# Norms between the stages of a two-layer encoder: other places for their rows, four buffers, an earlier transpose, a later weight load

## The chip, the core and the metric

The kernel runs on one core of a Trainium2 chip. The metric is the device time of one execution in microseconds; less is better. TensorE multiplies, VectorE and ScalarE do the elementwise work, GpSimd some of it, and SyncE issues most of the transfers. TensorE's clock has two levels here, 2.4 GHz (a granted clock of 1.00 in the profile) and 1.2 GHz (0.50).

## The reference

Two layers over 512 tokens of width 1024. Each layer has three parts, each behind a norm, each added to x. Layer 0 ends in a dense SwiGLU, layer 1 in eight experts of which each token takes two.

```python
for l in range(DEPTH):
    h = rms_norm(x, norm_mix[l])
    cols_a, cols_b, gate_a, gate_b = split_cols(h @ w_in[l], IN_SIZES)
    y_a, v_first = rwkv7_branch(cols_a, ...)      # time mixing, 8 heads
    y_b = dsa_attention(...)                      # top-128 sparse attention, 8 heads
    merged = (sigmoid(gate_a) * (y_a @ w_branch_a[l]) + sigmoid(gate_b) * (y_b @ w_branch_b[l]))
    x = x + merged @ w_out[l]
    x = x + memory_attention(rms_norm(x, norm_mem[l]), rms_norm(mem, mem_tok_norm[l]), ...)
    h = rms_norm(x, norm_ffn[l])
    x = x + (swiglu(h, ...) if l % 2 == 0 else moe_swiglu(h, router, bias, ...))
```

## The kernel before

Tokens lie in four tiles of 128 (`t` 0 to 3). Every float32 operand of a product is split into two float16 parts, a high one (`whi`, `hh`, `qhl`, `mh`, `oh`) and a low one (`wlo`, `hl`, `ml`, `ol`), and a product is three passes: low part of x times high of w, high times high, high times low. A weight tile goes through `wtile` (L251): SyncE loads it raw (L259), ScalarE casts the high part (L266), VectorE forms the low part (L271). Loads share a small ring of raw buffers, and SyncE takes its transfers in order: a transfer that waits for its place holds up the ones behind it.

`norm_T` (L167) is the norm between two stages. For each token tile ScalarE squares the rows of x and sums them (L182; the squares themselves go into the tile `xs` and are thrown away), VectorE and GpSimd make the scale factor `rs` (L164, L165), VectorE writes the scaled rows into the same `xs` (L187), and TensorE transposes them in 8 blocks of 128 by 128 into `pT` (L193), from which ScalarE and VectorE cast the two parts (L201, L202). `xs` has two buffers.

The stages around it, in order: `resid` (L1090) multiplies the merged branches (`mh`, `ml`) by w_out with `proj_tok` (L314, products at L331) and adds the result to x (L1096). `proj_tok` takes the last part of the weights token tile by token tile, so that x is complete for tile 0 first and for tile 3 last. `mem_attn` (L1156) then norms x, projects the queries of heads 0 and 1 with `proj_first` (L292, products at L301, the first 256 tokens ahead of the others), and runs the four heads; its output projection mem_wo adds to x at L1227. In layer 0 the projections of the memory tokens for layer 1 (`mem_kv`, weights mem_wkv) run in between. Then comes `ffn` (L1248) in layer 0 and `moe` (L1275) in layer 1, each with its norm. In `moe` the scaled rows are kept: `norm_T` puts them into tiles `row0` to `row3` of a pool, ScalarE makes their high part, GpSimd (VectorE for the last) the low part `rowl` (L1313), and `route` (L1381) makes the router's scores `plog`, the ranking `prk` and the gathering `px`.

The code is written as generators, and a scheduler orders each engine's instructions by their dependences and planned times; what the code fixes by hand, it fixes with `order` (L309): one instruction behind another on the same engine, without a wait. `self.hold`, where it is set, puts every weight load behind the load `self.lastw` of that moment. It is set to w_out's last load before the memory attention (L1739), and cleared after it.

Places in the on-chip memory are shared by pools that follow each other, and a tile that is laid on an older one waits until that one has been read. Before the change, in both layers, the second and the third raw buffer of the memory attention lie on `ml`, which w_out's products read to their end. The first of the expert layer's rows lies on `ol`, which mem_wo's products read to their end.

Of the kernel before, what the change touches and what calls it, by code (L numbers as in the profile page):

```python
# [8 lines left out]
F32 = mybir.dt.float32  # L9
# [3 lines left out]
F16 = mybir.dt.float16  # L13
# [6 lines left out]
P = 128  # L20
SEQ = 512
D = 1024
KT = 8
NT = 4
# [30 lines left out]
class Kern:  # L55
# [110 lines left out]

    def norm_T(self, xt, nt, targets, hd=None, rows=None, spread=False, gbs=None):  # L167

        nc = self.nc
        kept = []
        with self.tc.tile_pool(name="norm", bufs=2, side="right", reuse_waits="tile") as pn:
            gbs = gbs or [self.spread(g, f"gb{i}", pn) if spread else self.bcast_vec(g, D, f"gb{i}", pn)
                          for i, (g, _, _) in enumerate(targets)]
            for t in range(nt):
                ts = slice(t * P, (t + 1) * P)
                ssq = pn.tile([P, 1], F32, name="ssq")
                rs = pn.tile([P, 1], F32, name="rs")
                xs = pn.tile([P, D], F32, name="xs") if rows is None else rows.tile([P, D], F32, name=f"row{t}")  # L180
                kept.append(xs)
                nc.scalar.activation(xs, xt[:, t, :], AF.Square, accum_out=ssq)  # L182
                self.rstd(ssq, rs, 1, 1.0 / D, EPS)
                for i, (_, hi, lo) in enumerate(targets):
                    if i:
                        xs = pn.tile([P, D], F32, name="xs")
                    nc.vector.scalar_tensor_tensor(xs, xt[:, t, :], rs, gbs[i], OP.mult, OP.mult)  # L187
                    if hd is not None:
                        nc.scalar.dma_start(hd[ts, :], xs)
                    for q in range(2):  # L190
                        p = self.sm("pT")
                        for k in range(4):
                            nc.tensor.transpose(p[:, k * P:(k + 1) * P], xs[:, (4 * q + k) * P:(4 * q + k + 1) * P], self.ident)  # L193
                        ks = slice(4 * q, 4 * q + 4)
                        self.split_ps(hi[:, ks, ts], lo[:, ks, ts], p.rearrange("p (k t) -> p k t", k=4))
        return kept
# [117 lines left out]
    def proj_tok(self, pieces, xh, xl, nt, kt=KT, tail=1, tag="acc", kg=None):  # L314


        N = sum(p.shape[1] for p in pieces)
        kg = kg or max(1, 1024 // N)
        while kt % kg:
            kg -= 1  # L320
        ps = [self.bank(tag, "ptok") for _ in range(nt)]
        mm = self.nc.tensor.matmul
        groups = list(range(0, kt, kg))
        cut = max(0, len(groups) - tail)
        for part in [[k0] for k0 in groups[:cut]] + [groups[cut:]]:
            ws = [(k0, self.wtile([pc[k0 * P:(k0 + kg) * P, :] for pc in pieces], kg)) for k0 in part]
            for t in range(nt):
                ts = slice(t * P, (t + 1) * P)
                for k0, (hi, lo) in ws:
                    for k, x, w, first, last in self.passes(range(kg), xh, xl, hi, lo):  # L330
                        mm(ps[t][:, :N], lhsT=x[:, k0 + k, ts], rhs=w[:, k, :], start=k0 == 0 and first,  # L331
                           stop=k0 + kg == kt and last)
        return [p[:, :N] for p in ps]

# [718 lines left out]
    def branches(self, l, pool, G, ya, ybd, cx, ms):  # L1053


        nc, I = self.nc, self.I
        mf = self.hp.tile([P, KT, SEQ], F32, name="mf", tag="hl", bufs=1)
        for m in range(KT):
# [5 lines left out]
            yield  # L1064
        mp = cx.enter_context(self.tc.tile_pool(name="branch", bufs=1, reuse_waits="tile"))
        yb = mp.tile([P, 8, SEQ], F16, name="yb", tag="yb")
        for i in range(2):
            nc.sync.dma_start(yb[:, 4 * i:4 * i + 4, :], ybd[i].rearrange("j p t -> p j t"))
        ybl = [[yb[:, 4 * i + j, :] for j in range(4)] for i in range(2)]
        for m in range(KT):  # L1070
            tb = mp.tile([P, SEQ], F32, name="tb", bufs=3)
            nc.sync.dma_start(tb, G[8 + m])
            pb = self.proj_feat(I["w_branch_b"][l][:, m * P:(m + 1) * P], *ybl, 4)
            nc.vector.scalar_tensor_tensor(tb, tb, 1.0, pb, OP.add, OP.mult)
            nc.gpsimd.tensor_tensor(mf[:, m, :], mf[:, m, :], tb, OP.add)
            yield
# [3 lines left out]
        for m in range(KT):  # L1080
            ta = mp.tile([P, SEQ], F32, name="ta", bufs=7)
            nc.sync.dma_start(ta, G[m])
            pa = self.proj_feat(I["w_branch_a"][l][256:512, m * P:(m + 1) * P], [y[0] for y in ya[2:4]],
                                [y[1] for y in ya[2:4]], 2)
            nc.vector.scalar_tensor_tensor(ta, ta, 1.0, pa, OP.add, OP.mult)
            nc.vector.tensor_tensor(ta, ta, mf[:, m, :], OP.add)
            self.split_ps(mh[:, m, :], ml[:, m, :], ta, 0.5 / SW)
            yield
# [67 lines left out]
    def mem_attn(self, l, x, kv):  # L1156
# [5 lines left out]
        with self.more_weights(3, 3, 3), tc.tile_pool(name="mattn", bufs=1, reuse_waits="tile") as mp:  # L1162
            oh = mp.tile([P, 4, SEQ], F16, name="oh")
            ol = mp.tile([P, 4, SEQ], F16, name="ol")
            self.norm_T(x, NT, [(I["norm_mem"][l], hh, hl)])
            kT = mp.tile([P, 2, 4, 256], F16, name="akT")
# [81 lines left out]
    def ffn(self, l, x):  # L1248
        nc, I, tc = self.nc, self.I, self.tc
        hh = self.hp.tile([P, KT, SEQ], F16, name="fh", tag="hh", bufs=1)  # L1250
        hl = self.hp.tile([P, KT, SEQ], F16, name="fl", tag="hl", bufs=1)
        self.norm_T(x, NT, [(I["norm_ffn"][l], hh, hl)])
        j = l // 2
# [21 lines left out]
    def moe(self, l, x, out, c2, rawp):  # L1275
# [7 lines left out]
        with ExitStack() as cx:  # L1283
# [23 lines left out]
            ld[0] = itertools.chain([next(ld[0]) for _ in range(self.RAWS)], ld[0])  # L1307
            with self.psum(acc=4, sm=4), tc.tile_pool(name="router", bufs=1, reuse_waits="tile") as rp:
                hr = [rp.tile([P, NT, D], F16, name=f"row{c}") for c in "hl"]
                rows = self.norm_T(x, NT, [(I["norm_ffn"][l], hh, hl)], hd, rp)  # L1310
                for t, r in enumerate(rows):
                    a = nc.scalar.copy(hr[0][:, t, :], r).ins
                    (nc.vector if t == NT - 1 else nc.gpsimd).tensor_tensor(hr[1][:, t, :], r, hr[0][:, t, :], OP.subtract)  # L1313
                self.order(a, self.marks["hi"])
                self.marks["rows"] = a
                self.route(l, rp, hh, hl, hr, slot, gate, ovf, S7, XTs[0])
            with self.psum(acc=6, sm=2):
# [62 lines left out]

    def route(self, l, rp, hh, hl, hr, slot, gate, ovf, S7, XT):  # L1381

# [6 lines left out]
        sh = [P, NT, E]  # L1389
        rr = rp.tile([P, KT, E], F32, name="rr")  # L1390
        rs = rp.tile([P, KT, 2, E], F16, name="rs")
        rb = self.bcast_vec(I["moe_bias"][j], E, "rb", rp)
        nc.scalar.dma_start(rr, I["moe_router"][j].rearrange("(k p) e -> p k e", p=P))
# [302 lines left out]
    def layer(self, l, xsrc, xs):  # L1696
# [38 lines left out]
        with tc.tile_pool(name="memkv", bufs=1, side="right", reuse_waits="tile") as mp:  # L1735
# [6 lines left out]
            if l % 2 == 0:  # L1742
                self.mem_attn(l, x, kv)
                self.hold = None
        if l % 2:
# [10 lines left out]
        self.weights(*self.WB[2])  # L1756
        self.ffn(l, x)
        px.close()
        xd = self.dp.tile([SEQ, D], F32, name=f"xe{l}")
# [45 lines left out]
```

## Time and profile before

| | |
|---|---|
| median of 3 executions | 2080.55 us (2078.53 to 2082.65) |
| profiled execution | 2075.39 us, its span 2073.6 us |
| TensorE | busy 94% of the span, mean granted clock 0.959 |
| VectorE, ScalarE, GpSimd | busy 68%, 50%, 16% |

The times in the rows below are from the start of that span. Layer 0 ends its w_out at 564 and its memory attention near 660; layer 1 runs from there, with its w_out near 1526, its mem_wo near 1598, and the experts from 1620 to the end. The columns of each view are explained with its first group. In brackets at the end of a row of a timeline stands the idle time of that engine ahead of the row and what ended it.

### The profile page before, as it was taken

To read this page: it belongs to the slowest core of one execution; us is meant where nothing else is said; L and a number is where in the kernel's file an instruction comes from. 1 tells how busy PE (TensorE), PEld (TensorE's weight loads), DVE (VectorE), ACT (ScalarE), POOL (GpSimd) and SP (SyncE) were. 2 spreads that over 40 slices of the span, in tenths; PEclk is the share of its full clock that TensorE was granted. 3 is DMA by queue.
4 is the path that set the end of the run, shared out by engine and by line. 5 is a ranking of instruction groups with operands and counts; after the bars stand their busy time and mean duration, and the time that the engine had idled before them with its cause. 6 is when DMAs were issued, how large, how long until landed. Compare 5 with 4: busy or idle time off the path is not lost.

```text
span 2073.6 us, 40817 instructions
## 1 busy us (share of the span) xinstructions
PE 1940.1 (94%) x16760; PEld 1286.0 (62%) x16760; DVE 1413.4 (68%) x2373; ACT 1029.1 (50%) x1661; POOL 341.0 (16%) x357
## 2 busy tenths in 40 slices
PE   6998899899898999999998989979998899999997
PEld 3764565465465444444574546537455799999996
DVE  6766987756676333322466998574757888888886
ACT  5543446453453333322443435544335678888883
POOL 2260611003010000000243260100201310000002
PEclk9998999979999999999999999988999899999998
DMA  7334334325642333333434342434535699999993
GB/s 234 106 80 99 87 90 127 97 64 159 221 147 62 102 102 102 102 102 102 121 81 94 89 120 65 120 99 130 173 114 202 189 394 365 356 355 347 345 344 127
DMA packets 346742, 332.52 MB, mean 160 GB/s; under 512 B 101921, under 2 KB 263841, under 8 KB 346546
## 3 DMA queue, kind: packets, MB, share of 16 engines
q1 hardware_dynamic: 335440, 306.03, 47.2%
q10 hardware_dynamic: 8482, 15.39, 2.0%
q0 software_dynamic: 2624, 8.40, 1.2%
q8 instruction: 133, 2.18, 0.4%
q14 instruction: 63, 0.52, 0.1%
HBM read 297.05 MB, written 32.72 MB: 159 GB/s over the span
## 4 chain that ended last, share of the span: by engine, by line
PE 70%; DVE 12%; DMA 7%; ACT 3%; issue 3%; POOL 3%; SPq 2%; DVEq 0%; ACTq 0%; POOLq 0%
PE pf L289 23%; PE ptok L331 12%; PE pe L1567 10%; PE py L1612 6%; PE pSy L904 3%; PE pf L301 3%; PE ptok L349 2%; PE psc L527 1%; DVE wlo L271 1%; DMA eraw<-in_moe_wd_dram 1%; DVE iacc L518 1%; DVE pr L1003 1%; PE pA L808 1%; PE pT L193 1%; PE pp L558 1%
## 5 line engine op out<-in xcount | busy, mean ns | idle before, releaser
L266 ACT ACTIVATE whi<-raw 128x1024 f16<-128x1024 f32 (+2 forms) x244 | 227.7, 934 | 436.9 <-PE pf L289 187.3
L271 DVE SCALAR_TENSOR_TENSOR wlo<-raw,whi 128x1024 f16<-128x1024 f32 (+2 forms) x210 | 232.0, 1107 | 201.7 <-ACT whi L266 190.3
L1550 DVE SCALAR_TENSOR_TENSOR ewlo<-eraw,ewhi 128x1024 f16<-128x1024 f32 x265 | 321.1, 1220 | 58.0 <-ACT ewhi L1549 56.7
L289 PEld LDWEIGHTS <-whi 128*128 128x128 f16 x1888 | 182.5, 99 | 229.5 <-issue 34.8
L1549 ACT ACTIVATE ewhi<-eraw 128x1024 f16<-128x1024 f32 x265 | 277.4, 1054 | 77.9 <-PE py L1612 34.6
L1567 PE MATMUL pe<-XT,ewhi 128*128 128x144 f16 x2816 | 206.3, 226 | 1.7 <-issue 1.7
L1567 PEld LDWEIGHTS <-ewhi 128*128 128x128 f16 x2816 | 183.4, 98 | 2.3 <-issue 1.6
L289 PE MATMUL pf<-hh,whi 128*128 128x512 f16 x448 | 171.7, 383 | 2.6 <-DVE v L613 1.0
L289 PE MATMUL pf<-hl,whi 128*128 128x512 f16 x448 | 171.5, 383 | 0.0
L289 PEld LDWEIGHTS <-wlo 128*128 128x128 f16 x944 | 92.4, 99 | 112.0 <-issue 9.0
L269 POOL TENSOR_TENSOR wlo<-raw,whi 128x1024 f16<-128x1024 f32 (+3 forms) x34 | 59.9, 1761 | 596.1 <-ACT raw L268 512.9
L289 PE MATMUL pf<-fh,whi 128*128 128x512 f16 x336 | 127.3, 379 | 0.0
L289 PE MATMUL pf<-fl,whi 128*128 128x512 f16 x336 | 127.3, 379 | 0.0
L1567 PE MATMUL pe<-XT,ewlo 128*128 128x144 f16 x1408 | 117.2, 226 | 0.1
L289 PE MATMUL pf<-hh,wlo 128*128 128x512 f16 x448 | 112.6, 386 | 0.0
L1612 PE MATMUL py<-HT,ewhi 128*128 128x144 f16 x1408 | 103.9, 227 | 0.1
L1567 PEld LDWEIGHTS <-ewlo 128*128 128x128 f16 x1408 | 94.3, 98 | 0.8 <-issue 0.7
L1612 PEld LDWEIGHTS <-ewhi 128*128 128x128 f16 x1408 | 92.5, 98 | 0.3 <-issue 0.2
L289 PE MATMUL pf<-fh,wlo 128*128 128x512 f16 x336 | 79.4, 379 | 0.0
L349 PE MATMUL ptok<-whi,hh 128*128 128x256 f16 (+1 forms) x320 | 74.7, 274 | 2.1 <-ACT qe L485 2.0
L349 PE MATMUL ptok<-whi,hl 128*128 128x256 f16 (+1 forms) x320 | 75.0, 274 | 0.0
L349 PEld LDWEIGHTS <-hh 128*128 128x128 f16 x640 | 62.4, 100 | 15.5 <-issue 8.2
(462 smaller groups left out, 3879.3 us busy)
## 6 DMA issues: line engine op xcount, KB each, us to landing
raw<-in_w_in_dram SPq DMA_DIRECT2D x76, 512.0 KB, 4.0
eraw<-in_moe_wg_dram SPq DMA_DIRECT2D x16, 2048.0 KB, 12.9
eraw<-in_moe_wu_dram SPq DMA_DIRECT2D x16, 2048.0 KB, 14.3
eraw<-in_moe_wd_dram SPq DMA_DIRECT2D x16, 2048.0 KB, 12.9
eraw<-in_moe_wg_dram SPq DMA_DIRECT2D x8, 1536.0 KB, 11.9
eraw<-in_moe_wu_dram SPq DMA_DIRECT2D x8, 1536.0 KB, 14.6
eraw<-in_moe_wd_dram SPq DMA_DIRECT2D x8, 1536.0 KB, 8.5
raw<-in_ffn_wg_dram SPq DMA_DIRECT2D x22, 512.0 KB
```

Source lines behind the costliest of these rows:

```text
L266: nc.scalar.activation(hi, raw, AF.Copy, scale=SW)
L269: nc.gpsimd.tensor_tensor(lo, raw, hi, OP.subtract)
L271: nc.vector.scalar_tensor_tensor(lo, raw, SW, hi, OP.mult, OP.subtract)
L289: self.nc.tensor.matmul(p, lhsT=w[:, k, :], rhs=x[k], start=first, stop=last)
L301: m = self.nc.tensor.matmul(ps[i][:, cs], lhsT=w[:, k, :], rhs=x[k][:, cs], start=hf == 0 and start, stop=stop, skip_group_check=True)
L331: mm(ps[t][:, :N], lhsT=x[:, k0 + k, ts], rhs=w[:, k, :], start=k0 == 0 and first, stop=k0 + kg == kt and last)
L349: mm(p, lhsT=x[:, k0 + k, ts], rhs=w[:, k, :], start=k0 == 0 and t % 2 == 0 and first, stop=k0 + kg == kt and last, skip_group_check=True)
L904: m = mm(p[e][:, cc % 4, jj, :], lhsT=l, rhs=r, start=first[e] is None, stop=x == (1 if cc else 0), skip_group_check=True)
L1549: a = nc.scalar.activation(r[0], w, AF.Copy, scale=SW)
L1550: d = nc.vector.scalar_tensor_tensor(r[1], w, SW, r[0], OP.mult, OP.subtract)
L1567: mm(p[:, i * n:(i + 1) * n], lhsT=w[:, k, :], rhs=XT[:, k, h, :], start=z == 0, stop=z == len(ms) - 1)
L1612: mm(ps[d], lhsT=w[:, i, d * P:(d + 1) * P], rhs=HT[:, k, h, :], start=k == 0 and w is wh and h == 0 and d % per == 0, stop=k == FT - 1 an ...
```

## The change

- `norm_T` takes the number of `xs` buffers: four for the memory attention's norm in both layers and for the SwiGLU's norm in layer 0. It also takes `ahead`, instructions that are ordered behind the 8 transposes of the token tiles 0, 1, ... The memory attention gives it the first product of token tile 3 in w_out's last part (`self.tails[3:4]`, recorded by `proj_tok`).
- In `branches` the first of the tiles `tb` and `ta` are allocated ahead of `yb`, whose place `ml` takes later. `ml` thereby moves, and the raw buffers of the memory attention lie on `tb` and `ta`, which nobody reads by then.
- In `moe` the rows, their gain, and the router's tiles get a pool of their own on the right side. The gain vector `gbr` is loaded by SyncE behind the first four expert loads; it was loaded long before.
- `self.hold` isn't cleared after layer 0's memory attention but set to its last load, so that the SwiGLU's first weight loads stand behind mem_wo's.

```diff
-    def norm_T(self, xt, nt, targets, hd=None, rows=None, spread=False, gbs=None):
+    def norm_T(self, xt, nt, targets, hd=None, rows=None, spread=False, gbs=None, bufs=2, ahead=()):
...
-                xs = pn.tile([P, D], F32, name="xs") if rows is None else rows.tile([P, D], F32, name=f"row{t}")
+                xs = pn.tile([P, D], F32, name="xs", bufs=bufs) if rows is None else rows.tile([P, D], F32, name=f"row{t}")
...
-                            nc.tensor.transpose(p[:, k * P:(k + 1) * P], xs[:, (4 * q + k) * P:(4 * q + k + 1) * P], self.ident)
+                            m = nc.tensor.transpose(p[:, k * P:(k + 1) * P], xs[:, (4 * q + k) * P:(4 * q + k + 1) * P], self.ident)
+                        if t < len(ahead):
+                            self.order(ahead[t], m.ins)
...
+            self.tails = []
             for t in range(nt):
...
-                        mm(ps[t][:, :N], lhsT=x[:, k0 + k, ts], rhs=w[:, k, :], start=k0 == 0 and first,
+                        m = mm(ps[t][:, :N], lhsT=x[:, k0 + k, ts], rhs=w[:, k, :], start=k0 == 0 and first,
                            stop=k0 + kg == kt and last)
+                        if len(self.tails) == t:
+                            self.tails.append(m.ins)
...
+        tbs = [mp.tile([P, SEQ], F32, name="tb", bufs=3)]
+        tas = [mp.tile([P, SEQ], F32, name="ta", bufs=7)]
         yb = mp.tile([P, 8, SEQ], F16, name="yb", tag="yb")
...
-            tb = mp.tile([P, SEQ], F32, name="tb", bufs=3)
+            tb = tbs.pop() if tbs else mp.tile([P, SEQ], F32, name="tb", bufs=3)
...
-            ta = mp.tile([P, SEQ], F32, name="ta", bufs=7)
+            ta = tas.pop() if tas else mp.tile([P, SEQ], F32, name="ta", bufs=7)
...
-            self.norm_T(x, NT, [(I["norm_mem"][l], hh, hl)])
+            self.norm_T(x, NT, [(I["norm_mem"][l], hh, hl)], bufs=4, ahead=self.tails[3:4])
...
-        self.norm_T(x, NT, [(I["norm_ffn"][l], hh, hl)])
+        self.norm_T(x, NT, [(I["norm_ffn"][l], hh, hl)], bufs=4)
...
+                rwp = cx.enter_context(ExitStack())
+                rw = rwp.enter_context(tc.tile_pool(name="rows", bufs=1, side="right", reuse_waits="tile"))
+                gb = self.bcast_vec(I["norm_ffn"][l], D, "gbr", rw)
                 hr = [rp.tile([P, NT, D], F16, name=f"row{c}") for c in "hl"]
-                rows = self.norm_T(x, NT, [(I["norm_ffn"][l], hh, hl)], hd, rp)
+                rows = self.norm_T(x, NT, [(I["norm_ffn"][l], hh, hl)], hd, rw, gbs=[gb])
...
-                self.route(l, rp, hh, hl, hr, slot, gate, ovf, S7, XTs[0])
+                self.route(l, rp, rw, hh, hl, hr, slot, gate, ovf, S7, XTs[0])
+                rwp.close()
...
-        rr = rp.tile([P, KT, E], F32, name="rr")
-        rs = rp.tile([P, KT, 2, E], F16, name="rs")
-        rb = self.bcast_vec(I["moe_bias"][j], E, "rb", rp)
+        rr = rw.tile([P, KT, E], F32, name="rr")
+        rs = rw.tile([P, KT, 2, E], F16, name="rs")
+        rb = self.bcast_vec(I["moe_bias"][j], E, "rb", rw)
...
                 self.mem_attn(l, x, kv)
-                self.hold = None
+                self.hold = self.lastw
...
         self.ffn(l, x)
+        self.hold = None
```

TensorE at the end of w_out in layer 0, before: `ptok` are w_out's products for token tile 3, `pT` the transposes of the norm, `pf` the first query products.

```order
L331 LDWEIGHTS mh
L331 MATMUL ptok<-wlo,mh 128x512
L331 LDWEIGHTS mh
L331 MATMUL ptok<-wlo,mh 128x512
L193 MATMUL pT<-ct,xs 128x128 x24
L301 LDWEIGHTS whi
L301 MATMUL pf<-qhl,whi 128x256
```

The same place after: the last products of token tile 2, the transposes of tile 0, and the first products of tile 3.

```order
L334 LDWEIGHTS mh
L334 MATMUL ptok<-wlo,mh 128x512
L193 MATMUL pT<-ct,xs 128x128 x8
L334 LDWEIGHTS mh
L334 MATMUL ptok<-whi,mh 128x512
```

The transposes of tile 0 moved ahead of the 12 products of tile 3; behind these stand the 16 transposes of tiles 1 and 2, then 16 query products, then the 8 transposes of tile 3, where all of the first three tiles' transposes stood behind the products before.

ScalarE in the second half of layer 0's memory attention, before: `aq` is the last head's copy of its queries, `apr` its softmax, `oh` the head outputs, `whi<-raw` the cast of a weight tile.

```order
L204 ACTIVATE aqT<-pf 128x512
L204 ACTIVATE apT<-pmt 128x512 x2
L1178 ACTIVATE aq_6526<-pf 128x512
L204 ACTIVATE oh<-pmo 128x512
L1203 ACTIVATE apr,asm<-pms,amx,aqs 128x256 x2
L204 ACTIVATE apT<-pmt 128x512
L1203 ACTIVATE apr,asm<-pms,amx,aqs 128x256 x2
L266 ACTIVATE whi<-raw 128x512
```

The same place after; the casts of 128x1024 here are of the SwiGLU's first weights.

```order
L206 ACTIVATE aqT<-pf 128x512
L206 ACTIVATE apT<-pmt 128x512 x2
L268 ACTIVATE whi<-raw 128x1024
L1185 ACTIVATE aq_6526<-pf 128x512
L206 ACTIVATE oh<-pmo 128x512
L268 ACTIVATE whi<-raw 128x1024 x2
L1210 ACTIVATE apr,asm<-pms,amx,aqs 128x256 x4
L268 ACTIVATE whi<-raw 128x512
```

Three SwiGLU casts now stand here, ahead of the last head's query copy and softmax; before, they ran on ScalarE during w_out and the norm behind it. On SyncE the SwiGLU's loads stand behind the fifth load of mem_wo now, and the small loads of layer 1's constants (`mu` and others, L589) behind them; before, the SwiGLU's first five loads stood among those of w_out, mem_wq and mem_wkv.

VectorE in the middle of layer 1, inside the last inverse of the time mixing (`pr` and `tt` are its steps; L986, L987), before: `wlo` is the low part of a weight tile, `rv` the reciprocal of a softmax sum.

```order
L986 TENSOR_TENSOR pr<-tt_12566,Bt 128x49
L271 SCALAR_TENSOR_TENSOR wlo<-raw,whi 128x1024
L987 TENSOR_REDUCE tt_12566<-pr 128x7
L986 TENSOR_TENSOR pr<-tt_12566,Bt 128x64
L987 TENSOR_REDUCE tt_12566<-pr 128x8
L986 TENSOR_TENSOR pr<-tt_12566,Bt 128x81
L546 RECIPROCAL rv<-sme 128x4
```

The same steps after: `mf` is a gate product, `ybl` the low part of the sparse attention's output, the two lines of L546 one score pass of the sparse attention.

```order
L991 TENSOR_TENSOR pr<-tt_12566,Bt 128x49
L273 SCALAR_TENSOR_TENSOR wlo<-raw,whi 128x256
L992 TENSOR_REDUCE tt_12566<-pr 128x7
L1068 SCALAR_TENSOR_TENSOR mf<-gt,pf 128x512
L207 SCALAR_TENSOR_TENSOR ybl<-po,ybh 128x256
L991 TENSOR_TENSOR pr<-tt_12566,Bt 128x64
L546 ISA s_13045,mx<-psc,mask_9209 128x512
L546 ISA mx 128x1
L546 ISA s_13045,mx<-psc,mask_9209 128x512
L546 ISA mx 128x1
L992 TENSOR_REDUCE tt_12566<-pr 128x8
L991 TENSOR_TENSOR pr<-tt_12566,Bt 128x81
```

Gate products and score passes moved between the inverse's steps; before, most of them stood behind them.

## Rows read from the trace of the kernel before

**Rows 1.** The page, chain that ended last: share of the span by engine

```profile
PE 70%; DVE 12%; DMA 7%; ACT 3%; issue 3%; POOL 3%; SPq 2%; DVEq 0%; ACTq 0%; POOLq 0%
```

**Rows 2.** Timeline of TensorE at A: start, us, engine, line, operation, out<-in, count, idle before

```profile
564.03 1.91 PE L193 MATMUL pT<-ct,xs 128*128 128x128 f32 x16
569.64 1.94 PE L193 MATMUL pT<-ct,xs 128*128 128x128 f32 x8 [3.70 <-DVE xs L187]
...
579.16 0.38 PE L331 MATMUL ptok<-whi,memh 128*128 128x512 f16 x1
```

**Rows 3.** Windows: length, busy us (instructions) of PE, PEld, DVE, ACT, POOL; PEclk, DMA share, GB/s

```profile
568.00:569.00 1.00, 0.00 (x0) 0.00 (x0) 0.79 (x1) 1.00 (x3) 0.18 (x1) 0.50 0.94 332
...
574.00:575.00 1.00, 1.00 (x7) 0.74 (x6) 1.00 (x2) 0.00 (x0) 0.00 (x0) 0.61 0.92 244
...
636.00:640.00 4.00, 4.00 (x15) 2.04 (x13) 3.92 (x11) 1.83 (x6) 0.00 (x0) 0.57 0.62 132
```

**Rows 4.** Timeline of ScalarE at A: square of tile 2, a SwiGLU cast, two query casts

```profile
566.10 1.08 ACT L182 ACTIVATE xs<-x 128x1024 f32<-128x1024 f32 x1
...
567.15 1.06 ACT L266 ACTIVATE whi<-raw 128x1024 f16<-128x1024 f32 x1
...
569.62 2.14 ACT L266 ACTIVATE whi<-raw 128x1024 f16<-128x1024 f32 x2
```

**Rows 5.** Timeline of VectorE at A: second half of tile 2's sum, its scaled rows

```profile
561.80 0.68 DVE L1096 SCALAR_TENSOR_TENSOR x<-ptok,x 128x512 f32<-128x512 f32 x1
...
568.21 1.28 DVE L187 SCALAR_TENSOR_TENSOR xs<-x,rs,gb 128x1024 f32<-128x1024 f32 x1 [0.73 <-POOL rs L165]
```

**Rows 6.** Timelines of ScalarE and TensorE at D: query casts, transposes of tile 2

```profile
1530.80 2.02 ACT L266 ACTIVATE whi<-raw 128x1024 f16<-128x1024 f32 x2
...
1531.95 1.94 PE L193 MATMUL pT<-ct,xs 128*128 128x128 f32 x8 [3.87 <-DVE rs L164]
```

**Rows 7.** Timelines of all engines at E, from the last output product on

```profile
1598.18 1.06 ACT L182 ACTIVATE row<-x 128x1024 f32<-128x1024 f32 x1 [8.09 <-PE ptok L331]
...
1600.20 1.28 DVE L187 SCALAR_TENSOR_TENSOR row<-x,rs,gb 128x1024 f32<-128x1024 f32 x1 [0.69 <-POOL rs L165]
...
1601.63 1.42 PE L193 MATMUL pT<-ct,row 128*128 128x128 f32 x8 [3.54 <-DVE rs L164]
...
1604.06 2.64 POOL L1313 TENSOR_TENSOR rowl<-row,rowh 128x1024 f16<-128x1024 f32 x1 [1.36 <-ACT rowh L1312]
1607.18 5.20 POOL L1313 TENSOR_TENSOR rowl<-row,rowh 128x1024 f16<-128x1024 f32 x2
1607.24 3.14 DVE L187 SCALAR_TENSOR_TENSOR row<-x,rs,gb 128x1024 f32<-128x1024 f32 x1
...
1610.53 1.94 PE L193 MATMUL pT<-ct,row 128*128 128x128 f32 x8 [1.98 <-DVE lg L1403]
```

**Rows 8.** Timeline at C: a wait of VectorE, and TensorE's first row behind it

```profile
634.14 0.17 DVE L594 TENSOR_SCALAR mu<-mu 128x14 f32<-128x14 f32 x1 [3.12 <-DMA mu<-in_rwkv_mu_dram]
...
634.97 0.39 PE L331 MATMUL ptok<-whi,ol 128*128 128x512 f16 x1 [2.62 <-DVE ol L205]
```

**Rows 9.** Timeline of SyncE's queue: the five loads of mem_wo

```profile
605.68 17.53 SPq L259 DMA_DIRECT2D raw<-in_mem_wo_dram  x5
```

**Rows 10.** Timeline of layer 1's middle, around the last inverse

```profile
1364.84 0.68 DVE L541 CUSTOM_DVE_ANT_0 s<-psc,mask 128x512 f32<-128x512 f32 x1
...
1371.14 1.89 DVE L1003 TENSOR_TENSOR pr<-t1h,a 128x1024 f32<-128x1024 f32 x1 [5.62 <-DMA scrT<-tt]
...
1378.33 1.54 PE L558 MATMUL pp<-ct,s 128*128 128x128 f32 x6 [8.22 <-DVE mx L541]
...
1384.99 0.69 DVE L1063 SCALAR_TENSOR_TENSOR mf<-gt,pf 128x512 f32<-128x512 f32 x1 [0.63 <-DMA gt<-gatebuf]
```

**Rows 11.** Windows of layer 1's middle, ahead of the first scan

```profile
1200.00:1220.00 20.00, 13.04 (x82) 8.75 (x81) 19.34 (x41) 8.06 (x13) 11.20 (x13) 0.91 0.36 97
1220.00:1240.00 20.00, 18.07 (x138) 8.99 (x138) 19.74 (x43) 7.00 (x12) 14.32 (x13) 0.92 0.53 154
```

More of the change, by code (lines that the diff above doesn't have):

```diff
@@ L185, in norm_T @@
                     if i:
-                        xs = pn.tile([P, D], F32, name="xs")
+                        xs = pn.tile([P, D], F32, name="xs", bufs=bufs)
                     nc.vector.scalar_tensor_tensor(xs, xt[:, t, :], rs, gbs[i], OP.mult, OP.mult)
@@ L1379, in combine, with route @@
         return lambda: nc.vector.scalar_tensor_tensor(x[:, t, :], yr, gate, x[:, t, :], OP.mult, OP.add)
-    def route(self, l, rp, hh, hl, hr, slot, gate, ovf, S7, XT):
+    def route(self, l, rp, rw, hh, hl, hr, slot, gate, ovf, S7, XT):
         nc, I = self.nc, self.I
```

## The prediction

> **What bounds the kernel now.** I read the chain of work that ended last first. TensorE carries most of it [rows 1], so time is to be had only where TensorE stands still or runs at its lower clock. The second view was TensorE's idle time around the places that the change touches: the memory attention's norm in layer 0 (place A) and in layer 1 (place D), the second half of layer 0's memory attention (C), the dense SwiGLU's norm (B) and the expert layer's norm (E).
>
> At A, TensorE finishes 16 transposes at 565.9, then idles 3.70 us until VectorE has written the scaled rows of token tile 2 [rows 2]. Behind that idle time the granted clock was 0.50, the level of 1.2 GHz, and back at full about 574.8 [rows 3]; the stage ends at 579.16, where the next products start [rows 2]. What holds tile 2 back is its buffer. With two buffers, the squares of tile 2, which ScalarE writes into the buffer of tile 0, can't start before the transposes of tile 0 have read it, and these stand behind all of w_out's products. So the square starts at 566.10 [rows 4], though tile 2's sum was there 3.6 us before [rows 5]. D has the same shape with 3.87 us [rows 6]. E is another case: the square of the first row starts only after a wait of 8.09 us for the last product [rows 7], because the row's place lies on an operand of the output projection.
>
> **Place A, layer 0.** The change gives four buffers, puts tile 0's 8 transposes ahead of the last 12 products, and takes the SwiGLU's loads and casts away. Removed from the path: the SwiGLU's cast of 1.06 at 567.15 on ScalarE [rows 4] and one on VectorE. Added to TensorE ahead of the last products: 8 transposes at 1.91/16 each [rows 2], 0.95 us, which had to be done anyway, plus a wait of some 0.4 for tile 0's row. By hand, with the new orders and these durations: tile 0's transposes at 561.8, the last product at 565.4, tile 1's transposes to 566.4, tile 2's row at 566.9 in place of 568.21 [rows 5], its transposes at 568.2. But the cast of the first query weights now stands behind tile 3's square on ScalarE (1.08, and then half of 2.14 [rows 4]), so the first product can't run before about 570.4. TensorE still idles about 2.6 in all, and the stage ends at 576.7 if the clock holds, at 578.2 if it falls again. Elsewhere it fell to 0.57 behind an idle stretch of 2.62 [rows 3, 8], so I take a value nearer to the second: **gain 1.8**, bounds 0 and 6.2 (the whole 3.70, and half of the 5.0 us that TensorE then worked at the low clock).
>
> **Place C.** With the SwiGLU's loads behind mem_wo's, the next layer's constants move behind the SwiGLU's loads too. Their wait of 3.12 us on VectorE goes, and with it TensorE's 2.62 [rows 8] and about 1.7 that the clock of 0.57 over 4 us cost [rows 3]: up to 4.3 off the path. In its place come the SwiGLU's first casts. ScalarE's order now has one ahead of the last head's query copy and two ahead of its softmax (shown with the change). Each, 1.06 long, waits for a load, and none is issued before the fifth of mem_wo's, at 623.2 [rows 9]. I estimate that the first lands at 628 to 629, 2 to 3 us after the copy now runs, and the third, which must wait for a raw buffer, at 635. The copy, the head's scores and its softmax queue behind them. TensorE has other products to cover that, but not all of it: I put the new stalls at about 4.3 as well. **Net 0**, from -4.3 to +4.
>
> **Place B.** The SwiGLU's norm gets its buffers, but the transposes of its tiles 2 and 3 already lie among products: **0**, from -0.5 to +1.
>
> **Place D, layer 1.** As A without the SwiGLU's casts. The idle 3.87 ends on tile 2's row; its transposes end at 1533.9, and the cast of the query weights, at 1530.80, was ready by then [rows 6]. With tile 2's square free to run some 2 us earlier, the first product comes at about 1532. **Gain 1.9**, bounds 0 and 5.8 (the 3.87, and half of some 3.9 us of work at the low clock behind it, an estimate after A).
>
> **Place E.** The rows now lie on a place that nobody reads, so their squares run beside the output projection. VectorE must add the last output tile anyway before it turns to the rows, so row 0 (1.28) starts at most half a microsecond before its 1600.20 [rows 7]. The gain lies at row 3: GpSimd computed a low part (2.64) ahead of row 3's scale factor; now all four factors stand ahead of the three low parts. Row 3 can be scaled at about 1605 instead of 1607.24, and its transposes come at 1608.2 instead of 1610.53 [rows 7]. What follows, the router's scores and the ranking, moves up with it. The gain vector is now loaded behind four expert loads, into a place that the last head's softmax leaves, ahead of the output projection's end: nothing. **Gain 2.3**, bounds 0.4 and 5.5 (the idle 3.54 and 1.98 [rows 7]). The low end has this ground: row 3 took 3.14 beside GpSimd's low parts where row 0 alone took 1.28 [rows 7], and in the new order row 3 again runs beside them, and row 2 may, at up to 1.86 more.
>
> The Trainium skill (SBUF — State Buffer, "SBUF: two separate sides") says that VectorE and GpSimd share a pair of ports which one instruction holds to its end while the other is blocked. Taken strictly, row 3 would have waited out the first low part and taken 3.8; the row shows 3.14, so the trace agrees in direction and not in size. By the rule E comes out at its low end.
>
> **The middle of layer 1.** The diff doesn't name it, but the scheduler plans it anew: TensorE's order differs over some 2,000 products between 1020 and 1484. Two differences count. First, about 65 products of 512 columns stand earlier, ahead of the first scan, where TensorE was busy for only 13.04 and 18.07 of 20 us with VectorE full [rows 11]: up to 9 us of idle time could be filled. Second, the last inverse, a chain of VectorE steps and transfers that no TensorE work shortens. In it TensorE idled 8.22 us, while VectorE waited 5.62 for a transfer with a score pass queued behind the wait [rows 10]. In the new order eight gate products (0.69) and four score passes (0.68) [rows 10] stand among the inverse's 30 short steps, where two score passes stood: 8 x 0.69 + 2 x 0.68 is 6.9 us more ahead of the next transfer, with small casts up to 10. And TensorE has some 9 us less of other work to run meanwhile. In turn 96 products fill the scan behind it. The ends are about -10 and +12; I can't tell the sign, and take **0**.
>
> **Sum.** -1.8 + 0 + 0 - 1.9 - 2.3 + 0 = -6.0. Behind E lies the expert stage; its loads wait for buffers that E frees, so they start earlier with it and the gain passes on. The profiled execution took 2075.39 (its span 2073.6); it would become 2069.4. The median of the three times lies 5.16 above that execution, which I add: **2074.5**.
>
> **Rivals.**
> 1. *The freed time isn't kept.* The query weights' cast behind tile 3's square becomes what TensorE waits for at A and D, the clock falls in the same places, and C's late loads cost 2. For it: the order on ScalarE, and the 2.62 that sufficed for a fall. Against it: E doesn't depend on it. Sum: 0 - 0.5 - 1.5 + 2 = 0, 2080.5.
> 2. *Slower: the last inverse of layer 1.* With 6.9 to 10 us more on VectorE in the chain, and less work to cover it, TensorE waits 20 us or more ahead of the last pY instead of 8. It decides if VectorE's added passes don't fall into its waits for transfers. For it: the orders. Against it: the work placed earlier. Price 10 to 12, with the norms' -6: 2084.5 to 2086.5; if C adds 2, 2088.
> 3. *The middle gains.* The 65 products fill the idle 9 us under a full VectorE, and the inverse's added passes lie in waits: 9 less, 2065.5.
> 4. *The shared ports at E.* GpSimd's low parts hold up row 3 by 1.9 us: 2076.4.
>
> **How the numbers follow.** A measurement of this kernel tells about 0.2% (4.2 us) from no change: faster is below 2076.4, slower above 2084.7. The forecast has a chance of 0.38 (nearly all faster), rival 1 0.23 (same), rival 2 0.22 (slower), rival 3 0.12 (faster), rival 4 0.05 (half faster, half same). Faster 0.51, same 0.27, slower 0.22. The range reaches from rival 3 with A's full bound, 2061, to rival 2's upper end, 2088; the forecast's own range is 2070 to 2078.
>
> **What would show it.** Right: at A, tile 2's transposes within 2.5 us of tile 1's; at D, less than 2.5 us idle; at E, row 3's transposes 2 us earlier, counted from the last output product; at C, no VectorE wait on the constants; in layer 1's middle, no longer way from the last pB to w_out's first product. Wrong: a low clock at A and D as long as before; ScalarE waiting on a SwiGLU load ahead of the last softmax with TensorE idle behind it; an idle stretch of over 12 us ahead of the last pY.

## The result and the profile of the changed kernel

The changed kernel takes 2096.68 us (median of 6 runs, 2094.39 to 2098.43), the kernel before 2079.45 beside it. The ratio is 1.0083, 95% interval 1.0070 to 1.0096: slower by 17.2 us. The profiled execution took 2098.43, its span is 2096.6.

By the starts of the same instructions in both traces, the whole loss lies in the middle of layer 1, from its first score product to w_out's first product. The products `pB` go into the last inverse, and `pY` are the first that use its result.

| stretch | before | after |
|---|---|---|
| w_out of layer 0 to the first SwiGLU product (A, C, B) | 146.0 | 144.9 |
| layer 1: first score product to the last `pB` | 247.0 | 260.2 |
| last `pB` to the first `pY` behind the last inverse | 61.8 | 65.3 |
| first `pY` to layer 1's w_out | 84.8 | 94.7 |
| w_out to the first query product (D) | 49.5 | 48.5 |
| last mem_wo product to the gathering `px` (E) | 23.4 | 22.7 |

The middle is 26.5 us longer, the rest 3.5 shorter. Each figure is from one execution; differences below 1 us say little (D took 49.5 in the kernel before and 50.3 in a kernel with the same code there, the one with later constants below). The windows of its three parts, of before and then of after, columns as in [rows 3]:

```profile
1090.58:1337.55 246.97, 230.69 (x1757) 131.99 (x1757) 204.38 (x433) 110.55 (x218) 72.07 (x75) 0.97 0.38 99
...
1337.55:1399.34 61.79, 49.41 (x286) 23.17 (x283) 41.80 (x96) 29.86 (x68) 4.83 (x6) 0.89 0.38 94
1399.34:1484.16 84.82, 81.42 (x797) 54.28 (x797) 51.70 (x95) 34.19 (x76) 17.35 (x13) 0.90 0.43 135
```

```profile
1088.92:1349.11 260.19, 245.02 (x1843) 138.14 (x1844) 212.70 (x447) 122.59 (x245) 72.15 (x76) 0.97 0.37 99
...
1349.11:1414.39 65.28, 45.22 (x280) 23.63 (x276) 43.96 (x96) 29.74 (x65) 3.47 (x5) 0.77 0.40 93
1414.39:1509.05 94.66, 79.49 (x717) 54.08 (x718) 41.46 (x80) 22.78 (x52) 17.59 (x13) 0.80 0.32 96
```

TensorE runs the same 2,840 instructions in both. Its busy time rises by 8.2 us (361.5 to 369.7, the lower clock: 0.77 and 0.80 in the last two parts) and its idle time by 18.4 (16.3 + 12.4 + 3.4 to 15.2 + 20.1 + 15.2). The first part holds 86 instructions and 14.3 us of TensorE work more, while its idle time falls by 1.1 only. The two later parts hold 86 instructions fewer, but at the lower clock only 6.1 us of work less.

The last inverse on VectorE, after: its first step, three waits for gate loads inside, its last step, and the wait for its result's transfer (before: [rows 10]).

```profile
1357.75 0.16 DVE L991 TENSOR_TENSOR pr<-tt,Bt 128x1 f32<-128x1 f32 x1 [5.35 <-DMA Bt<-scrA]
...
1367.52 0.69 DVE L1068 SCALAR_TENSOR_TENSOR mf<-gt,pf 128x512 f32<-128x512 f32 x1 [1.30 <-DMA gt<-gatebuf]
...
1369.32 0.69 DVE L1068 SCALAR_TENSOR_TENSOR mf<-gt,pf 128x512 f32<-128x512 f32 x1 [0.39 <-DMA gt<-gatebuf]
...
1375.12 0.69 DVE L1068 SCALAR_TENSOR_TENSOR mf<-gt,pf 128x512 f32<-128x512 f32 x1 [0.46 <-DMA gt<-gatebuf]
...
1379.89 0.39 DVE L992 TENSOR_REDUCE tt<-pr 128x15 f32<-128x225 f32 x1
...
1390.73 1.88 DVE L1008 TENSOR_TENSOR pr<-t1h,a 128x1024 f32<-128x1024 f32 x1 [3.80 <-DMA a<-scrA]
```

The steps take 22.5 us; before they ran from 1345.58 to 1358.93, 13.35 us. Most of these 9.2 us are made up again: from the last step to the first `pY` it is 34.1 us, before 40.4, so that the part from the last `pB` to the first `pY` is only 3.5 longer. TensorE's two longest waits in the middle, ahead of the first `pY` and at the end of the scan:

```profile
1414.39 0.31 PE L1033 MATMUL pY<-TN,AM 32*32 32x32 f32 x2 [6.70 <-DMA TN<-scrN]
...
1487.57 1.97 PE L947 MATMUL pyT<-ct,yc 64*64 64x64 f32 x32 [5.95 <-DVE yc L941]
```

The page's chain has less TensorE and more VectorE than [rows 1]:

```profile
PE 67%; DVE 16%; DMA 6%; ACT 3%; issue 3%; POOL 2%; SPq 2%; ACTq 0%; DVEq 0%; POOLq 0%
```

Places A and D on TensorE, after ([rows 2, 6] before), and the windows that answer to [rows 3]:

```profile
562.50 1.06 PE L193 MATMUL pT<-ct,xs 128*128 128x128 f32 x8 [0.29 <-DVE rs L164]
...
567.34 1.06 PE L193 MATMUL pT<-ct,xs 128*128 128x128 f32 x8 [0.31 <-DVE xs L187]
...
570.60 1.92 PE L303 MATMUL pf<-qhl,whi 128*128 128x256 f16 x16 [2.19 <-ACT whi L268]
```

```profile
1554.35 1.06 PE L193 MATMUL pT<-ct,xs 128*128 128x128 f32 x8 [0.40 <-DVE xs L187]
...
1557.52 1.92 PE L303 MATMUL pf<-qhl,whi 128*128 128x256 f16 x16 [2.10 <-ACT whi L268]
```

```profile
568.00:569.00 1.00, 0.40 (x4) 0.16 (x2) 0.99 (x2) 1.00 (x2) 0.00 (x0) 1.00 0.88 348
574.00:575.00 1.00, 1.00 (x12) 0.90 (x10) 1.00 (x3) 1.00 (x2) 0.00 (x0) 1.00 0.71 231
632.00:636.00 4.00, 4.00 (x17) 2.42 (x18) 2.64 (x5) 0.36 (x1) 1.56 (x1) 0.50 0.82 241
```

At A the clock stays at 1.00; at C it still falls, now to 0.50. ScalarE at C, the first and the third SwiGLU cast, and what TensorE then waits for:

```profile
628.79 1.06 ACT L268 ACTIVATE whi<-raw 128x1024 f16<-128x1024 f32 x1 [4.59 <-DMA raw<-in_ffn_wg_dram]
...
635.64 1.06 ACT L268 ACTIVATE whi<-raw 128x1024 f16<-128x1024 f32 x1 [3.87 <-DMA raw<-in_ffn_wg_dram]
```

```profile
630.39 1.80 PE L1188 MATMUL pss<-ones,aq 128*128 128x2 f32 x8 [4.33 <-ACT aq L1185]
```

Place E: the scaling of rows 0 and 1, that of row 3, the second half of row 2's transposes, which waits for a low part on VectorE, and the second half of row 3's ([rows 7] before):

```profile
1621.75 2.48 DVE L187 SCALAR_TENSOR_TENSOR row<-x,rs,gbr 128x1024 f32<-128x1024 f32 x2 [0.63 <-POOL rs L165]
...
1626.82 2.55 DVE L187 SCALAR_TENSOR_TENSOR row<-x,rs,gbr 128x1024 f32<-128x1024 f32 x1
...
1630.03 1.11 PE L193 MATMUL pT<-ct,row 128*128 128x128 f32 x4 [1.73 <-DVE el L204]
...
1632.34 1.09 PE L193 MATMUL pT<-ct,row 128*128 128x128 f32 x4
```

The low part on GpSimd that runs when row 3 is scaled, before and after:

```profile
1607.18 2.12 POOL L1313 TENSOR_TENSOR rowl<-row,rowh 128x1024 f16<-128x1024 f32 x1
```

```profile
1625.45 2.84 POOL L1323 TENSOR_TENSOR rowl<-row,rowh 128x1024 f16<-128x1024 f32 x1
```

### The profile page after: what moved, and what is told of

Its sections match the earlier page's. It is cut to its first block, busy times and chain, and to the rows that moved or that the text cites. A ratio compares the mean times of both kernels' runs of the same rounds, so it can differ in the third digit from the quotient of the medians.

```text
span 2096.6 us, 40816 instructions
## 1 busy us (share of the span) xinstructions
PE 1948.6 (93%) x16760; PEld 1291.5 (62%) x16760; DVE 1411.2 (67%) x2373; ACT 1029.7 (49%) x1661; POOL 340.4 (16%) x357
## 4 chain that ended last, share of the span: by engine, by line
PE 67%; DVE 16%; DMA 6%; ACT 3%; issue 3%; POOL 2%; SPq 2%; ACTq 0%; DVEq 0%; POOLq 0%
PE pf L291 20%; PE pe L1578 12%; PE ptok L334 11%; PE py L1623 6%; PE pSy L909 3%; PE pf L303 2%; DVE iacc L523 2%; PE ptok L354 2%; DVE wlo L273 2%; DVE m L522 1%; DVE pr L1008 1%; PE psc L532 1%; DMA raw<-in_w_out_dram 1%; PE pA L813 1%; ACT whi L268 1%
```

## The experiments

**Is it the plan of layer 1's middle?** The first kernel is the changed one with the order of every engine in layer 1's middle held to that of the kernel before, by `order` alone. The second is the kernel before with the changed kernel's order there. (Holding the middle without the hold of the loads, in the second and in those built on the third below, also puts six small VectorE steps on layer 1's constants behind the SwiGLU's norm.)

```diff
+    def pin(self, ins):
+        for e, plan in self.PLAN.items():
...
+            for a, b in zip(run[1:], run):
+                self.order(a, b)
...
+            if l == 1:
+                self.pin(list(self.nc.cur_bb.bb.instructions)[n0:])
```

> The whole change, but in layer 1 from its first norm to the branches every engine is held to the order of the kernel before (one instruction behind another, no added wait). Theory 'plan': the loss of 17 us against before is the newly planned order of layer 1's middle, which shows 18.4 us more idle time and 8.1 us more at the low clock than before there; outside of it the trace of after is 4 us shorter. So this kernel takes 2075 to 2077, 2 to 5 below before, and the way from the last pB to w_out's first product is 146 to 148 us as before. Rival 'places': the moved tiles and loads themselves hold the middle up (transfers that wait for their places); then the same order waits in the same places and the time stays above 2088.

Measured: 0.9969 (0.9954 to 0.9984), 2076.81 us; its middle takes 398.1 us.

> The kernel before with nothing of the change, but with layer 1's middle held to the order that the changed kernel has there. Theory 'plan': the loss comes along with the order: before plus 24 to 28 us, 2103 to 2108, and the idle stretches ahead of the last pY (6.7) and behind the scan (about 6) are there. Rival 'places': the order alone costs nothing, within 5 us of before.

Measured: 1.0080 (1.0061 to 1.0099), 2097.14 us; its middle takes 418.0 us, 393.6 before, 420.1 after. The 2103 to 2108 expected left out the gain from the constants' steps, which move here too. The three parts of its middle:

```profile
1084.95:1345.96 261.01, 246.07 (x1843) 138.33 (x1844) 212.69 (x447) 122.63 (x245) 71.22 (x76) 0.97 0.36 99
1345.96:1411.60 65.64, 44.44 (x280) 22.85 (x276) 43.59 (x96) 29.62 (x65) 3.58 (x5) 0.83 0.40 92
1411.60:1502.95 91.35, 76.90 (x716) 52.48 (x717) 41.44 (x79) 22.76 (x52) 17.58 (x13) 0.82 0.34 106
```

The loss is the new order of a stage in which the change itself touches only the places of two tiles, and the first kernel has these places and not the loss. All else together gains 0.3%.

**The hold of the loads.** The third kernel, against the first:

```diff
-                self.hold = self.lastw
+                self.hold = None
```

> As the first, but the SwiGLU's loads stand early again, as before (the hold is cleared behind the memory attention). Against the first kernel of this call, by my prediction's terms: place A loses the SwiGLU's casts' removal again (about +0.5 to +1 there) and place C gets back its wait on the constants: together -1 to +2 us. If the SwiGLU's casts ahead of the last softmax cost what I feared (+4), this one is faster than the first by 2 to 4.

Measured: 0.9936 (0.9920 to 0.9951), 2069.50 us, faster than both. w_out to the SwiGLU takes 140.4 in place of 144.8. TensorE's wait at C in the first kernel, which this one doesn't have:

```profile
629.57 1.87 PE L1188 MATMUL pss<-ones,aq 128*128 128x2 f32 x8 [4.56 <-ACT aq L1185]
```

Where the gain of this version comes from is shown by the kernel before, its middle held to its own order, with only the constants' steps behind the last row that the SwiGLU's norm scales (`behind`):

```diff
-        nc.vector.tensor_scalar(mu1, mu, -1 / SW, 1 / SW, OP.mult, OP.add)
+        m = nc.vector.tensor_scalar(mu1, mu, -1 / SW, 1 / SW, OP.mult, OP.add)
+        if l:
+            self.order(m.ins, self.behind)
...
+        self.behind = self.scaled
```

> The kernel before with one thing changed: VectorE's six small steps on layer 1's constants stand behind the SwiGLU's norm instead of inside layer 0's memory attention (layer 1's middle is held to the order of before). By my term for place C this takes away the wait of 3.12 with TensorE's 2.62 idle and 1.7 us of the low clock: 4 to 5 us faster than before. If the wait only passes to the next transfer or load, within 1 us of before.

Measured: 0.9978 (0.9962 to 0.9994), 4.6 us less; the stretch to the SwiGLU takes 141.0 in place of 146.0. About a third of the third kernel's 0.64% is this wait of [rows 8].

**Without holding the middle.** Against the changed kernel, again only without the hold of the loads:

> Branch places, four row buffers, early transposes and the new order of loads as in the change, without its hold of the constants, and without holding layer 1's middle: the planner lays that stage anew. Theory 'the plan makes the loss': the new plan of the middle costs 10 to 25 us against the held one, so the kernel is at 2080 to 2095, ratio 1.000 to 1.008. If the loss had been the constants' hold and not the plan, it would be at about 2069 (0.994) as with the order held.

Measured: 1.0066 (1.0048 to 1.0084); its middle takes 426.0 us. The gain needs the held order. Which part upsets the planner? The third kernel again, with its middle held to the orders that the planner makes for two sets of parts: four buffers with the hold, and the early transposes alone.

> As e3 (the change without the later SwiGLU loads), but layer 1's middle held to a third order, which the scheduler makes from four buffers and later SwiGLU loads alone. By TensorE's work at full clock, 8 us more stand ahead of the last pB than in the order of before (20 in the changed kernel's), and the 96 products of the sparse attention's output lie inside the scan as in the changed kernel. Theory 'cover used up early': what is taken ahead of the last inverse is missing behind it; the middle becomes 6 to 13 us longer than in e3, between it and the changed kernel's +26. Rival 'only the changed kernel's own order is bad': within 3 us of e3.

Measured: 1.0013 (0.9998 to 1.0028), middle 407.0, 11.2 more than the third kernel's 395.8.

> As e3, but layer 1's middle held to a fourth order, which the scheduler makes from the earlier transposes alone: 9 us more of TensorE's work ahead of the last pB, but from the last pY on everything stands as in the order of before. If the time from the last pB to the last pY can't be shortened by giving TensorE less to do there, the middle becomes 6 to 9 us longer than in e3. If the loss of the changed kernel is made behind pY alone (products inside the scan), it stays within 2 us of e3.

Measured: 1.0051 (1.0030 to 1.0072), middle 421.8, 26 more where 6 to 9 were expected. Several parts disturb the plan, each in its own way, and I couldn't price such a plan from its order.

One thing is common to all new orders. Up to the last `pB` the middle takes 246.6 to 248.6 us in the kernel before and in every kernel held to its order, and 260.2 to 272.7 in the six traces with another order. From there to the first `pY` it is 59.8 to 61.8 with the old order, and with the others anything from 58.4 to 69.8.

**Which part of the new order costs?** The changed kernel with its own order, but the 30 inverse steps in a row (the table's orders here and below written out by the names of the tiles):

```diff
...
-                DVE: pr, wlo, tt, mf, ybl, pr, s, s, tt, pr
+                DVE: pr, tt, pr, tt, pr, wlo, mf, ybl, s, s
...
```

> The changed kernel with its own plan, but VectorE's 30 steps of the last inverse stand in a row again; the gate products and score passes that the plan had put between them come behind them. Theory 'the lengthened inverse': its 22.5 us go back to about 13.4, the waits ahead of the first pY become shorter, and the time falls by 4 to 9 us against the changed kernel (2088 to 2093). Rival 'cover used up ahead': the products moved ahead are still missing behind the inverse and the displaced passes are late instead, so the time stays within 2 us of the changed kernel (2095 to 2099).

Measured: 1.0108 (1.0090 to 1.0126), nothing gained against the changed kernel's 1.0083. The steps take 9.1 us, but the passes that TensorE waits for now stand behind them, and the result isn't sent: its transfer stands on SyncE behind six weight loads and seven gate loads. The first of these waits for the low part of a weight, most of the gate loads for a gate product, and these passes are now behind the inverse. TensorE, VectorE's last step, and SyncE (1386.44 less 1369.61: the result lay 16.8 us):

```profile
1370.87 0.48 PE L843 MATMUL pV<-ct,v 128*128 128x128 f32 x1 [8.82 <-ACT UV L856]
```

```profile
1369.22 0.39 DVE L992 TENSOR_REDUCE tt<-pr 128x15 f32<-128x225 f32 x1
```

```profile
1372.70 1.25 SPq L261 DMA_DIRECT2D raw<-in_w_branch_a_dram  x2
...
1383.78 2.13 SPq L1065 DMA_DIRECT2D gt<-gatebuf  x2
1386.00 0.39 SPq L261 DMA_DIRECT2D raw<-in_w_branch_b_dram  x1
1386.44 0.50 SPq L993 DMA_DIRECT2D scrB<-tt  x1
```

So I moved the transfers and the second steps ahead as well:

```diff
...
-                SP: gt, raw, gt, raw, gt, gt, raw, scrB, scrT, t1h, t2f, a
+                SP: scrB, scrT, t1h, t2f, a, gt, raw, gt, raw, gt, gt, raw
...
```

> The changed kernel with its own plan, but the whole way of the last inverse is put ahead of what was mixed into it: on VectorE its 30 steps in a row and the second steps with one other pass behind each; on SyncE its result's transfer ahead of the gate loads, and the last transfers ahead of the last loads of w_branch_b. Theory 'the way of the inverse': the first pY comes 5 to 12 us earlier than in the changed kernel, counted from the last pB (58 to 64 in place of 65.3), and the kernel takes 2085 to 2092. Rival 'cover': VectorE has the same passes to do ahead of the pY whatever their order (50 us with 7.5 idle), and TensorE the same products, so the idle time only moves to the passes that are now late: 64 to 75 us from the last pB to the first pY, and 2094 to 2107.

Measured: 1.0115 (1.0081 to 1.0149), by four executions, none of which has a trace. Neither variant is faster than the changed kernel, so shortening the inverse alone gives nothing back. That VectorE and TensorE have the same work ahead of the first `pY` in any order, with less cover, agrees with it, but isn't shown. Which products would have to move back wasn't tried one by one, so it stays open which part of the new order costs.

**The norms, one part at a time, against the third kernel** (0.9936, 0.9920 to 0.9951). Each ratio is against the kernel before on the same chip, but the chips differ, so only the ratios compare.

The first query weights' cast ahead of the last square:

```diff
...
+            self.order(self.squares[-1], self.casts[n])
```

> As e3, but ScalarE casts the first query weights ahead of the square of token tile 3, in both layers. By my prediction TensorE's remaining idle time at places A and D (2.8 in e3's layer 0, ended by this cast) hangs on it: 1 to 2 us less at each place, so 2 to 4 us below e3, about 2065. Rival: the next wait, on tile 2's transposes and casts, stands right behind: within 1 us of e3.

Measured: 0.9943 (0.9923 to 0.9964). The idle time at A falls from 2.78 to 1.74 + 0.55, at D from 2.11 to 1.20; the time doesn't show it.

The expert rows on their old places:

```diff
-                rows = self.norm_T(x, NT, [(I["norm_ffn"][l], hh, hl)], hd, rw, gbs=[gb])
+                rows = self.norm_T(x, NT, [(I["norm_ffn"][l], hh, hl)], hd, rp)
...
```

> As e3, but the expert layer's rows, gain and router tiles lie where they lay before (row 0 on the output projection's operand). By my prediction's term for place E (2.3, bounds 0.4 and 5.5) it is 2.3 us slower than e3; by the rival 'shared ports' only 0.4 slower.

Measured: 0.9967 (0.9951 to 0.9984); E takes 23.2, with the new places 22.6. The trace gives the rows 0.6 us; the rest of the difference isn't in the stretch that the edit changes.

The branches' tiles on their old places:

```diff
-        tbs = [mp.tile([P, SEQ], F32, name="tb", bufs=3)]
-        tas = [mp.tile([P, SEQ], F32, name="ta", bufs=7)]
...
```

> As e3, but with the places of the branches' tiles as before, so that the second and third raw buffer of the memory attention lie on an operand of w_out again and the query weights' loads wait for w_out's end. By the terms for A and D, which hang on the early cast of the query weights, it is 2 to 4 us slower than e3. Rival: the cast waits for tile 3's square anyway, so the later load costs under 1 us.

Measured: 0.9943 (0.9925 to 0.9961), idle 2.78 and 2.10 as with the new places: the cast stands behind the square anyway, and the time shows nothing that an earlier load buys.

No early transposes:

```diff
-            self.norm_T(x, NT, [(I["norm_mem"][l], hh, hl)], bufs=4, ahead=self.tails[3:4])
+            self.norm_T(x, NT, [(I["norm_mem"][l], hh, hl)], bufs=4)
```

> As e3, but tile 0's transposes stand behind all of w_out's products again; with four buffers the squares of tiles 2 and 3 don't wait for them. If the four buffers carry the gain at A and D, within 1 us of e3; if the early transposes do (0.95 us of TensorE's work at each place taken into the products), 1 to 2 us slower.

Measured: 0.9926 (0.9909 to 0.9944), 2068.38 us, the lowest figure of all, but not clear of the third kernel's. And this with the cast ahead of the square:

> Layer 1's middle held to the old order; four row buffers, the new branch places and the new order of loads, no early transposes, no hold of the constants, and on ScalarE the cast of the first query weights ahead of the square of tile 3. If the two idle gaps at the memory norms are what is left there, they fall below 1 us each and the time is at or up to 2 us below that without early transposes (2066 to 2069, ratio about 0.992). If they are covered anyway, no difference (ratio 0.9925 to 0.994).

Measured: 0.9936 (0.9919 to 0.9952), no difference. Two buffers in place of four in all three norms, in the first kernel and in the third (there with the constants' steps still behind the SwiGLU's norm):

```diff
-            self.norm_T(x, NT, [(I["norm_mem"][l], hh, hl)], bufs=4, ahead=self.tails[3:4])
+            self.norm_T(x, NT, [(I["norm_mem"][l], hh, hl)], bufs=2, ahead=self.tails[3:4])
...
-        self.norm_T(x, NT, [(I["norm_ffn"][l], hh, hl)], bufs=4)
+        self.norm_T(x, NT, [(I["norm_ffn"][l], hh, hl)], bufs=2)
```

> As the first, but with two buffers of scaled rows in both norms instead of four. The early transposes of tile 0 free its buffer ahead of the last 12 products, so tile 2's square can start early all the same: by this theory within 1 us of the first kernel at places A and D. If the four buffers carry the gain, A and D idle 3.7 and 3.9 again and it is 2 to 4 us slower than the first.

Measured: 0.9986 (0.9973 to 0.9998), where the first kernel has 0.9969.

> As e3, but with two buffers of scaled rows; layer 1's constants are held behind the SwiGLU's norm as they are in e3. With the early transposes the first two buffers come free ahead of the last 12 products. If that is enough, within 1 us of e3; if the four buffers carry the gain, 2 to 4 us slower.

Measured: 0.9958 (0.9941 to 0.9975). Both pairs put four buffers some 0.2% ahead, within their intervals, and the traces don't bear it out. With two, once the transposes are early, TensorE idles 1.19 + 0.46 us at A and 1.20 + 0.46 at D in the first kernel, with four 0.30 + 2.19 and 0.40 + 2.10; D takes 46.9 us with two and 47.9 with four. That four buffers gain anything beside the early transposes is not shown.

## Why the prediction was wrong

**The step that failed is "the middle of layer 1: 0".** I had its bounds, -10 to +12, and it was +26.5. Two readings under it fell.

- *Idle TensorE time taken for room.* I let 65 products fill up to 9 us of idle time [rows 11]. Between 1200 and 1240 they filled about half of it: TensorE's idle time there fell from 8.9 us to 4.7. But behind 1240 it rose from 0.3 to 3.2, and the part ahead of the last `pB` as a whole got 14.3 us more TensorE work and became 13.2 longer. VectorE was full between 1200 and 1240 before [rows 11] and after, and the moved products brought 8.3 us of VectorE work along (204.38 to 212.70 in the whole part); that this is why no more was filled is argued, not shown. The moved work would have paid only if the later parts had become as much shorter, and they became 13.3 longer. The windows, the last of before and then two of after:

```profile
1240.00:1337.55 97.55, 97.26 (x860) 61.21 (x857) 74.95 (x180) 51.99 (x122) 12.31 (x11) 1.00 0.33 94
```

```profile
1200.00:1240.00 40.00, 35.31 (x184) 18.56 (x183) 39.51 (x79) 16.68 (x24) 26.23 (x26) 0.96 0.46 125
1240.00:1349.11 109.11, 105.94 (x955) 64.58 (x954) 79.87 (x193) 60.60 (x147) 9.93 (x9) 1.00 0.33 98
```

- *A price for one leg, none for what lies around it.* Rival 2 named the place: 6.9 to 10 us more on the inverse (measured 9.2), and 20 us of TensorE waiting ahead of the `pY` (20.1; before 12.4, of which the 8.22 was one wait). But it put the whole price, 10 to 12, on this leg, which became only 3.5 longer, and no single wait there exceeds 6.70, where the sign for it was 12. It left out the work used up ahead (+13.2) and the end of the scan (+9.8), where 717 instructions are left in place of 797, TensorE waits 15.2 in place of 3.4, and the clock falls. So the range ended at 2088, and rival 2's right direction is partly luck. The leg by itself doesn't carry the loss: with the steps in a row, nothing came back.

**The other steps** hold in the main by the traces, with one size wrong, E, and some luck at C.

- *A*: the first query product was set at about 570.4; it came at 570.60, with w_out begun 0.70 later. The clock stayed at 1.00, as the gain's upper part supposed.
- *C*: the first SwiGLU cast at 628.79 (628 to 629 estimated), the third at 635.64 (635), a stall of 4.33 (4.3). The prediction gave no working for its 4.3, so that agreement is luck. The net 0 hid two large terms: alone, the constants gained 4.6 us, and the hold costs 0.33%, some 7 us by the times and 4.4 by the traces (144.8 to 140.4), about the stall.
- *Layer 0's memory attention in all*: 1.1 shorter, 1.8 forecast. Two errors nearly cancel: at the last product of the memory tokens the changed kernel was 3.1 us ahead (96.4 us behind w_out's start, before 99.6), more than A's 1.8, and from there it lost 2.0, where C was put at 0.
- *D*: 1.0 shorter here, 1.8 with the middle held, 1.9 forecast; the query cast ends the wait, as said.
- *E*: mis-sized, 0.7 in place of 2.3. Row 0 was scaled 0.5 earlier behind the last output product (1619.57 here), row 3 2.5 earlier (7.25 behind it, 9.74 before). But row 3 again took 2.55 beside GpSimd, which is rival 4's mechanism, and the second half of row 2's transposes waited 1.73 for a low part queued behind row 3's scaling on VectorE; row 3's transposes stand behind that. The transposes end 13.86 behind the last product, 14.97 before. The low bound, 0.4, had named this ground. In both traces row 3's scaling ends 1.08 us behind the low part on GpSimd that ran when it started. The prediction's 3.8 took that low part as 2.6 us long; it took 2.12, so waiting it out would have given 3.3, and the 3.14 is near that.

The forecast of -6 for the norms was too large by the traces: A to E are 2.8 shorter, all outside the middle 3.5, with the hold against it. By the times the change with the old order in the middle gains 6.4 us (3.3 to 9.6), which has -6 in it. The gain was lost to a stage that I left at zero because I couldn't tell its sign.
